# Cached keys stored head channel first by the host: attention and memory keys loaded in place instead of transposed on the tensor engine

## The chip, the cores and the metric

The kernel runs on one core of one Trainium2 chip. The metric is device time in microseconds (us) of one execution; smaller is better. The host may lay out the inputs as it likes before the launch, and that is not timed. Engines are named as in the profile: PE (TensorE, with PEld for its weight loads), DVE (VectorE), ACT (ScalarE), POOL (GpSimd) and SP (SyncE), whose queue issues most DMAs.

## The reference, cut to what matters

One layer of a streaming encoder on two groups of tokens: a prompt of 2048 frames (16 tiles of 128 rows), and 8 short streams ("samples") of 16 new frames each, together one more tile of 128 rows. Only the samples have caches, and their keys are what the change is about.

```python
# mixer attention of a sample: 256 cached frames + 16 new ones, 8 heads x 64
k_ext = concat([past_k, k]);  v_ext = concat([past_v, v])
s = einsum("bqhd,bkhd->bhqk", q, k_ext) * 64**-0.5 + bias
p = softmax(s);  att = einsum("bhqk,bkhd->bqhd", p, v_ext)

# cross-attention of a sample into its 256 cached memory tokens, 4 heads x 256
s = einsum("bthd,bmhd->bhtm", h @ w_mq, cache_mem_k) * 256**-0.5
o = einsum("bhtm,bmhd->bthd", softmax(s), cache_mem_v)
```

Both scores contract over the head channel d. A PE matmul contracts over the 128 partitions, so the keys have to lie with d on the partitions and the cached frames along the row. The caches come with frames first: cache_att_k is 8 x 256 frames x 512 channels, cache_mem_k is 8 x 256 tokens x 1024 channels.

## The kernel before, in words

The phases follow each other: memory keys and values of the prompt, projections with the convolution (`phase_proj`), prompt attention (`attention`), output projection (`mixout`), cross-attention (`phase_cross`), and the feed-forward layers. The whole program passes through a scheduler that plans with costs of its own and sets the order on each engine, so the order on an engine isn't that of the code; each engine then runs its row of instructions strictly in that order, and SP's DMA issues are such a row too.

SBUF is cut by hand into regions. A `Region` gives a tag its places, and `t(...)` walks round them. Two regions matter here. `att_pools` lays the samples' tiles from 34.5 KB of the arena `sbF`: `kc` (2 x 4 KB, raw keys), `kt` (1 x 4.25 KB, transposed keys with 16 new columns), `pp`, `vn` (1 x 2 KB). In the same arena the projection phase keeps the convolution's inputs `ut` (six slots of 3.125 KB from 26 KB; the last group's four channel blocks j = 0 to 3 take the slots at 32.25, 35.375, 38.5 and 41.625 KB) and `us`, the samples' conv input (44.75 to 50.5 KB, a quarter for each j). So the first loads of the attention phase wait for the last taps of the convolution, on DVE (`conv_vector`, L523) for `ut`, on ACT (L532) for `us`.

`attention` runs 8 heads x 16 tiles ("units"). A unit has score matmuls (L861), a fused bias-and-maximum on DVE (L793), the exponential on ACT (L795), transposes of the probabilities on PE (L878) with eviction and split on ACT and DVE (L879, L880), and after each four units the value matmuls (L891). Beside head h runs `sample(h)` as filler, one step at every second unit: load keys, values and new values (L800, L802, L804); eight PE transposes of 128x128 in two steps (L812), each four evicted by an ACT copy (L813); the new frames' keys by POOL (L815); score matmuls (L826); softmax; transposes of the probabilities (L835); value matmuls with 32 columns (L844, L845).

`mixout` multiplies 17 tiles by w_out as products of split fp32 (high and low part, three matmuls each, helper `mm3h`, L291). Beside it `cross_sample` runs as filler: query projection; then 16 jobs of keys (8 samples x 2 halves of the heads), then 16 jobs of values, then the output projection. `Ahead` makes each job two ahead of its use. A key job before: the first half's job loads both 128-token blocks of the sample (two tiles `wf`, 512 KB each, L1091); per block four transposes (L1170) into PSUM, a high part by an ACT cast from PSUM (L1172), a low part by a DVE subtraction of it from PSUM (L1173); then eight score matmuls (L1189). A value job needs no transpose: `split(load(...))` loads 512 KB into `wf`, casts it on ACT (L1085) and subtracts on DVE (L1086), both from SBUF.

Of the kernel before, what the change touches and what calls it, by code (L numbers as in the profile page):

```python
# [17 lines left out]
P = 128  # L18
D = 1024
# [6 lines left out]
NM = 256  # L26
# [3 lines left out]
DEC_B = 8  # L30
DEC_S = 16
PAST = 256
# [104 lines left out]
class Build:  # L137
# [610 lines left out]

    def att_pools(self):
        sbF, sbR, fa, fb = self.sbF, self.sbR, self.fa, self.fb  # L750
        self.attp = (Region().lay(sbF, 34.5, ("kc", 4, 2), ("kt", 4.25, 1), ("pp", 1.5, 1), ("vn", 2, 1))
                     .at("z", 2.5, (fa, [24]), (fb, [0, 2.5, 5]), (fa, [9, 11.5, 14, 16.5]))
                     .lay(fb, 7.5, ("vc", 4, 2), ("nmx", 0.03125, 12), ("sm", 0.03125, 2))
                     .lay(fa, 0, ("qbd", 2.5, 2), ("otmp", 2, 1), ("bs", 1.0625, 1)).lay(fa, 19, ("bt", 2.5, 2))
                     .lay(sbR, 0, ("q20", 8, 1), ("k20", 8, 1), ("kl0", 8, 1), ("q21", 8, 1), ("k21", 8, 1), ("kl1", 8, 1),
                          ("v20", 8, 1), ("ph1", 10, 1), ("pl1", 10, 1), ("v21", 8, 1))
                     .lay(sbR, 88, ("ph0", 10, 1), ("pl0", 10, 1)))
# [25 lines left out]
    def attention(self):  # L783
        nc, A = self.nc, self.A
# [11 lines left out]
            return z  # L796

        def sample(s):
            kc = self.t(pool, [P, 2, 512], F32, "kc", 2)
            nc.sync.dma_start(kc[:, :, :], A["cache_att_k"][s].rearrange("(b p) d -> p b d", p=P))  # L800
            vc = self.t(pool, [P, 2, 512], F32, "vc", 2)
            nc.sync.dma_start(vc[:, :, :], A["cache_att_v"][s].rearrange("(b p) d -> p b d", p=P))  # L802
            vn = self.t(pool, [DEC_S, 512], F32, "vn", 2)
            nc.sync.dma_start(vn[:, :], self.vsamp[s * DEC_S:(s + 1) * DEC_S, :])  # L804
            yield
            kt = self.t(pool, [P, 4, PAST + DEC_S], F32, "kt", 1)
            for c2 in range(0, 4, 2):
                pt = self.t(ps_t, [P, 2, 2, P], F32, "t")
                for c in range(2):
                    for b in range(2):  # L810
                        cc = slice((c2 + c) * P, (c2 + c + 1) * P)
                        nc.tensor.transpose(pt[:, c, b, :], kc[:, b, cc], self.ident[:, :])  # L812
                nc.scalar.copy(kt[:, c2:c2 + 2, :PAST].rearrange("p c (b k) -> p c b k", k=P), pt[:, :, :, :])  # L813
                yield
            nc.gpsimd.tensor_copy(kt[:, :, PAST:], self.ksamp[:, :, s * DEC_S:(s + 1) * DEC_S])  # L815
            yield
            qb = qbds[s % 2]
            for o in range(2):
                rr = slice(o * DH, (o + 1) * DH)
                nc.vector.tensor_copy(qb[rr, :, o * DEC_S:(o + 1) * DEC_S],  # L820
                                      self.qsamp[rr, :, s * DEC_S:(s + 1) * DEC_S])
            qb = qb[:, :, :].rearrange("p c x -> p (c x)")
            n = PAST + DEC_S
            ps = self.t(ps_s, [P, 2, 512], F32, "s")[:, 0, :n]
            for c in range(4):
                nc.tensor.matmul(ps, qb[:, c * P:(c + 1) * P], kt[:, c, :], start=c == 0, stop=c == 3)  # L826
            sm = self.t(pool, [P, 1], F32, "sm", 2)
            z = softmax_band(ps, n, bs[:, :], sm[:, :])
            nc.vector.reciprocal(sm[:, :], sm[:, :])
            nc.gpsimd.tensor_scalar(z[:, :n], z[:, :n], sm[:, :], None, ALU.mult)  # L830
            yield
            pt = self.t(ps_t, [P, 3, P], F32, "t")
            for b in range(3):
                w = P if b < 2 else DEC_S
                nc.tensor.transpose(pt[:w, b, :], z[:, b * P:b * P + w], self.ident[:, :])  # L835
            pp = self.t(pool, [P, 3, P], F32, "pp", 1)
            nc.scalar.copy(pp[:, :2, :], pt[:, :2, :])
            nc.scalar.copy(pp[:DEC_S, 2, :], pt[:DEC_S, 2, :])
# [230 lines left out]
    def cross_sample(self, pool, ps_so, ps_p):  # L1069
# [19 lines left out]
        def load(src):  # L1089
            wf = self.t(pool, [P, D], F32, "wf")  # L1090
            nc.sync.dma_start(wf[:, :], src)  # L1091
            return wf
# [63 lines left out]

        z = self.t(pool, [P, MH, NM], F32, "sh", 1)
        jobs = [(s, b) for s in range(DEC_B) for b in range(2)]
        kcs = {}

        def keys(s, half):
            if half == 0:
                kcs[s] = [load(A["cache_mem_k"][s, b * P:(b + 1) * P, :]) for b in range(2)]
            kh = self.t(pool, [P, 4, NM], F32R, "kvh")
            kl = self.t(pool, [P, 4, NM], F32R, "kvl")
            for b in range(2):
                bs = slice(b * P, (b + 1) * P)
                pt = self.t(ps_p, [P, 4, P], F32, "p")
                for k in range(4):
                    nc.tensor.transpose(pt[:, k, :], kcs[s][b][:, (4 * half + k) * P:(4 * half + k + 1) * P],  # L1170
                                        self.ident[:, :])
                nc.scalar.copy(kh[:, :, bs], pt[:, :, :])  # L1172
                nc.vector.tensor_tensor(kl[:, :, bs], pt[:, :, :], kh[:, :, bs].bitcast(F32), ALU.subtract)  # L1173
            return kh, kl

        ahead = Ahead([lambda j=j: keys(*j) for j in jobs])
        pd = pad(0, qT)
# [1 line left out]
        for x, (s, half) in enumerate(jobs):  # L1179
            kh, kl = next(ahead)  # L1180
            cur = pd
# [4 lines left out]
            for k in range(4):  # L1186
                kk = 4 * half + k
                for y, r in enumerate((kh, kl)):
                    nc.tensor.matmul(sc[:, kk // 2, :], cur[:, kk, :], r[:, k, :],  # L1189
                                     start=s % 4 == 0 and kk % 4 == 0 and y == 0,  # L1190
                                     stop=s % 4 == 3 and kk % 4 == 3 and y == 1, skip_group_check=True)
            if half == 1 and s % 4 == 3:
# [454 lines left out]
def layout(inputs):  # L1647
# [8 lines left out]
    o["cache_att_k"] = i["cache_att_k"].reshape(DEC_B, PAST, 512)  # L1656
    o["cache_att_v"] = i["cache_att_v"].reshape(DEC_B, PAST, 512)
    o["cache_conv"] = i["cache_conv"].reshape(DEC_B * HALO, 512)
    o["cache_mem_k"] = i["cache_mem_k"].reshape(DEC_B, NM, D)
    o["cache_mem_v"] = i["cache_mem_v"].reshape(DEC_B, NM, D)  # L1660

    def colblocks(w):
# [39 lines left out]
```

## Time and profile before

| | |
|---|---|
| median of three runs | 3033.25 us (3031.68 to 3037.04) |
| profiled execution | 3033.59 us, its span 3031.8 us |
| PE busy | 2949.8 us (97%), PEld 2715.4 us (90%) |
| DVE, ACT, POOL busy | 2138.1 (71%), 1357.7 (45%), 1397.0 us (46%) |
| mean granted PE clock | 0.987 of full speed |
| DMA | 500.08 MB, 165 GB/s over the span |

In windows of the profile a row gives, for a stretch of time, each engine's busy us with its instruction count, then the granted clock, the busy share of the 16 DMA engines, and GB/s. In groups and lines of instructions a row gives line, engine, operation, output<-input, count, busy time and mean ns of one, and what ended the idle time before it. A matmul record's length has a pipeline tail in it, so the busy time of a group of back-to-back matmuls divided by their count gives their pace, and the mean of one doesn't.

### The profile page before, as it was taken

The numbers are of one execution on the slowest core, as the hardware profiler recorded it, in microseconds if no ns is written. First come the engines' busy times: TensorE is split into PE (matmuls) and PEld (weight loads), VectorE is DVE, ScalarE is ACT, GpSimd is POOL, SyncE is SP. The second block draws the span as 40 slices with busy tenths as digits, with TensorE's granted clock in tenths as the row PEclk, the third lists the DMA queues.
The fourth block names the chain that finished last, engine by engine and source line by source line (L and its number), as shares of the span: only waits on it lengthen the run. The fifth ranks groups of instructions, "written<-read, shape, count | busy, mean of one in ns | idle before, by whom it ended". The sixth has DMA issues, their size and how long they took to land.

```text
span 3031.8 us, 45992 instructions
## 1 busy us (share of the span) xinstructions
PE 2949.8 (97%) x16924; PEld 2715.4 (90%) x16924; DVE 2138.1 (71%) x3077; ACT 1357.7 (45%) x2718; POOL 1397.0 (46%) x1304
## 2 busy tenths in 40 slices
PE   8999999979999999999999999999999999999998
PEld 8999999969997888787888999999999999888786
DVE  6696895957775466535357887888788998656655
ACT  4545454757784345323234333433334444433433
POOL 0267495710012234325356655555555776424413
PEclk9999999989999999999999999999999999999999
DMA  8635255557753556324246433544334446756654
GB/s 300 245 110 188 87 161 163 169 142 182 170 145 134 176 183 227 125 66 144 78 167 216 138 133 119 180 161 160 139 130 153 145 139 208 255 172 208 222 196 163
DMA packets 196429, 500.08 MB, mean 165 GB/s; under 512 B 18981, under 2 KB 82989, under 8 KB 187875
## 3 DMA queue, kind: packets, MB, share of 16 engines
q1 hardware_dynamic: 185883, 461.09, 47.3%
q0 software_dynamic: 10320, 36.05, 3.1%
q8 instruction: 133, 2.18, 0.3%
q14 instruction: 93, 0.76, 0.1%
HBM read 365.97 MB, written 141.81 MB: 167 GB/s over the span
## 4 chain that ended last, share of the span: by engine, by line
PE 40%; DMA 3%; DVE 3%; POOL 2%; issue 1%; ACT 1%; SPq 0%; DVEq 0%; POOLq 0%; ACTq 0%
PE psb L285 13%; PE psb L284 13%; PE psb L283 13%; DMA sbf<-in_w_down_dram 1%; PE psb L291 1%; DMA sbf<-x 1%; POOL sbf L1553 1%; DVE sbr L1614 1%; PE psb L1408 1%; DMA sbf<-hn 0%; DVE sbr L1431 0%; POOL sbf L340 0%; DMA hn<-sbf 0%; DVE flexb L1493 0%; DMA sbf<-in_w_gate_dram 0%
## 5 line engine op out<-in xcount | busy, mean ns | idle before, releaser
L283 PE MATMUL psb<-sbr 128*128 128x384 f32 (+3 forms) x2808 | 943.3, 337 | 4.4 <-ACT sbr L1613 1.4
L284 PE MATMUL psb<-sbr 128*128 128x384 f32 (+3 forms) x2356 | 806.8, 343 | 2.7 <-DVE sbr L320 2.4
L285 PE MATMUL psb<-sbr 128*128 128x512 f32 (+3 forms) x1848 | 633.2, 344 | 3.5 <-DVE sbr L1614 3.4
L283 PEld LDWEIGHTS psb<-sbr 128*128 128x128 f32 x2808 | 531.2, 189 | 34.4 <-ACT sbr L1613 2.8
L285 PE MATMUL psb<-sbr,sbx 128*128 128x384 f32 (+2 forms) x1484 | 477.8, 323 | 0.0
L284 PEld LDWEIGHTS psb<-sbr 128*128 128x128 f32 x2356 | 445.8, 189 | 29.8 <-DVE sbr L320 2.7
L285 PEld LDWEIGHTS psb<-sbr 128*128 128x128 f32 x1848 | 348.1, 189 | 33.3 <-DVE sbr L1614 6.6
L291 PE MATMUL psb<-sbr 128*128 128x512 f32 x1200 | 296.1, 395 | 6.4 <-DVE sbr L1019 1.7
L1431 DVE TENSOR_TENSOR sbr<-sbf,sbr 128x512 fp32r<-128x512 f32 x258 | 263.1, 1023 | 39.7 <-ACT sbr L1430 38.8
L1430 ACT CAST sbr<-sbf 128x512 fp32r<-128x512 f32 x258 | 159.3, 620 | 276.9 <-PE psb L284 231.0
L285 PEld LDWEIGHTS psb<-sbr,sbx 128*128 128x128 f32 x1484 | 281.5, 190 | 0.2
L291 PEld LDWEIGHTS psb<-sbr 128*128 128x128 f32 x1200 | 222.8, 189 | 52.9 <-DVE sbr L1019 1.9
L523 DVE SCALAR_TENSOR_TENSOR psb<-sbf,psb 128x768 f32<-128x768 f32 (+1 forms) x290 | 264.3, 911 | 6.2
L1614 DVE TENSOR_TENSOR sbr<-sbf,sbr 128x384 fp32r<-128x384 f32 (+1 forms) x231 | 170.8, 762 | 94.0 <-ACT sbr L1613 92.1
L278 POOL TENSOR_TENSOR sbx<-sbf,sbr 128x1024 fp32r<-128x1024 f32 x60 | 151.6, 2529 | 80.7 <-ACT sbr L277 77.2
L1613 ACT CAST sbr<-sbf 128x384 fp32r<-128x384 f32 (+1 forms) x231 | 111.0, 497 | 168.3 <-PE psb L284 153.7
L1553 POOL TENSOR_TENSOR sbf<-sbf 128x512 f32<-128x512 f32 x77 | 108.0, 1407 | 167.9 <-DMA sbf<-in_w_down_dram 166.1
L533 POOL TENSOR_TENSOR flexb<-flexb,flexb 128x128 f32<-128x128 f32 (+1 forms) x180 | 169.4, 941 | 22.3 <-ACT flexb L532 12.8
L283 PE MATMUL psb<-sbr,sbx 128*128 128x384 f32 (+1 forms) x524 | 170.6, 327 | 1.6 <-ACT sbx L1430 0.9
L1430 ACT CAST sbx<-sbf 128x512 fp32r<-128x512 f32 x153 | 94.7, 621 | 162.4 <-PE psb L284 150.6
L1431 DVE TENSOR_TENSOR sbx<-sbf,sbx 128x512 fp32r<-128x512 f32 x153 | 152.3, 997 | 15.9 <-ACT sbx L1430 15.5
L277 ACT CAST sbr<-sbf 128x1024 fp32r<-128x1024 f32 x98 | 102.7, 1051 | 107.2 <-PE psb L284 57.6
(336 smaller groups left out, 6246.9 us busy)
## 6 DMA issues: line engine op xcount, KB each, us to landing
af<-flexb SPq DMA_DIRECT2D x33, 1344.0 KB, 6.0
sbf<-in_w_down_dram SPq DMA_DIRECT2D x154, 256.0 KB, 3.8
sbf<-af SPq DMA_DIRECT2D x90, 384.0 KB, 3.9
sbf<-in_w_gate_dram SPq DMA_DIRECT2D x66, 512.0 KB, 3.4
sbf<-in_w_up_dram SPq DMA_DIRECT2D x66, 512.0 KB, 3.4
sbf<-x SPq DMA_DIRECT2D x49, 512.0 KB, 3.9
sbf<-in_w_in_dram SPq DMA_DIRECT2D x48, 512.0 KB, 4.1
sbr<-ks SPq DMA_DIRECT2D x28, 512.0 KB, 10.2
```

What stands on the lines that cost most here:

```text
L278: self.lo_engine.tensor_tensor(lo[:, :], wf[:, :], hi[:, :].bitcast(F32), ALU.subtract)
L283: nc.tensor.matmul(ps, lh, rh, start=start, stop=False, **kw)
L284: nc.tensor.matmul(ps, lh, rl, start=False, stop=False, **kw)
L285: nc.tensor.matmul(ps, ll, rh, start=False, stop=stop, **kw)
L291: nc.tensor.matmul(y[o], l, r[:, o * 512:(o + 1) * 512], start=start and x == 0, stop=stop and x == 2)
L523: nc.vector.scalar_tensor_tensor(acc if w < CW - 1 else o, src(w), cwt[:, j, w:w + 1], acc, ALU.mult, ALU.add)
L533: nc.gpsimd.tensor_tensor(o, o, v, ALU.add)
L1430: nc.scalar.copy(hs[j][:, :], src[j])
L1431: nc.vector.tensor_tensor(ls[j][:, :], src[j], hs[j][:, :].bitcast(F32), ALU.subtract)
L1553: nc.gpsimd.tensor_tensor(acc[:, :], acc[:, :], q[:, :], ALU.add if s > 0 else ALU.subtract)
L1613: nc.scalar.copy(ch[:, m], a[:, x, m])
L1614: nc.vector.tensor_tensor(cl[:, m], a[:, x, m], ch[:, m].bitcast(F32), ALU.subtract)
```

## The change: what it does

The host writes the cached keys with the channels first. cache_att_kt[s] is 128 channels x (4 channel blocks x 256 frames); cache_mem_kt[s, half] is 128 channels x (4 channel blocks x 256 tokens). The kernel loads them straight into the place where the transposes used to put them.

```diff
-        self.attp = (Region().lay(sbF, 34.5, ("kc", 4, 2), ("kt", 4.25, 1), ("pp", 1.5, 1), ("vn", 2, 1))
+        self.attp = (Region().lay(sbF, 34.5, ("kt", 4.25, 2), ("pp", 1.5, 1), ("vn", 2, 2))
...
         def sample(s):
-            kc = self.t(pool, [P, 2, 512], F32, "kc", 2)
-            nc.sync.dma_start(kc[:, :, :], A["cache_att_k"][s].rearrange("(b p) d -> p b d", p=P))
+            kt = self.t(pool, [P, 4, PAST + DEC_S], F32, "kt", 2)
+            nc.sync.dma_start(kt[:, :, :PAST], A["cache_att_kt"][s].rearrange("p (c k) -> p c k", k=PAST))
...
             yield
-            kt = self.t(pool, [P, 4, PAST + DEC_S], F32, "kt", 1)
-            for c2 in range(0, 4, 2):
-                pt = self.t(ps_t, [P, 2, 2, P], F32, "t")
-                for c in range(2):
-                    for b in range(2):
-                        cc = slice((c2 + c) * P, (c2 + c + 1) * P)
-                        nc.tensor.transpose(pt[:, c, b, :], kc[:, b, cc], self.ident[:, :])
-                nc.scalar.copy(kt[:, c2:c2 + 2, :PAST].rearrange("p c (b k) -> p c b k", k=P), pt[:, :, :, :])
-                yield
             nc.gpsimd.tensor_copy(kt[:, :, PAST:], self.ksamp[:, :, s * DEC_S:(s + 1) * DEC_S])
...
         def keys(s, half):
-            if half == 0:
-                kcs[s] = [load(A["cache_mem_k"][s, b * P:(b + 1) * P, :]) for b in range(2)]
-            kh = self.t(pool, [P, 4, NM], F32R, "kvh")
-            kl = self.t(pool, [P, 4, NM], F32R, "kvl")
-            for b in range(2):
-                bs = slice(b * P, (b + 1) * P)
-                pt = self.t(ps_p, [P, 4, P], F32, "p")
-                for k in range(4):
-                    nc.tensor.transpose(pt[:, k, :], kcs[s][b][:, (4 * half + k) * P:(4 * half + k + 1) * P],
-                                        self.ident[:, :])
-                nc.scalar.copy(kh[:, :, bs], pt[:, :, :])
-                nc.vector.tensor_tensor(kl[:, :, bs], pt[:, :, :], kh[:, :, bs].bitcast(F32), ALU.subtract)
-            return kh, kl
+            return split(load(A["cache_mem_kt"][s, half])[:, :])
...
-                    nc.tensor.matmul(sc[:, kk // 2, :], cur[:, kk, :], r[:, k, :],
+                    nc.tensor.matmul(sc[:, kk // 2, :], cur[:, kk, :], r[:, k * NM:(k + 1) * NM],
```

The `kt` tile now has two places and receives the DMA itself, in 1 KB pieces (a row of 256 frames; the tile's rows are 272 long), where `kc` came in 2 KB pieces. `vn` has two places too. `sample` has two filler steps fewer. The lines behind the cut move up: L826 is L817 in the new kernel, L861 L852, L878 L869, L891 L882, L1085 and L1086 are L1076 and L1077, L1189 is L1167.

The scheduler plans anew from the cut on. First place: PE in the key jobs beside `mixout` (L291 is w_out, L1170 the transposes, L1189 the scores). Before:

```order
L1170 MATMUL psb<-ident_73,sbf 128x128 x4
L1189 MATMUL psb<-flexb_8732 128x256 x7
L1189 MATMUL psb<-sbr,flexb_8732 128x256
L291 MATMUL psb<-sbr 128x512
L965 MATMUL psb<-ident_73,sbr 16x128
L1189 MATMUL psb<-sbr,flexb_8732 128x256 x7
L291 MATMUL psb<-sbr 128x512 x3
L1170 MATMUL psb<-ident_73,sbf 128x128 x4
L291 MATMUL psb<-sbr 128x512
L291 MATMUL psb<-sbr,sbx 128x512 x7
```

And now (L1167 is L1189 of before, L956 is L965):

```order
L956 MATMUL psb<-ident_73,sbr 16x128
L291 MATMUL psb<-sbr 128x512 x12
L1167 MATMUL psb<-flexb_8652 128x256 x8
L291 MATMUL psb<-sbr 128x512 x6
L1167 MATMUL psb<-sbr,flexb_8652 128x256 x8
L291 MATMUL psb<-sbr 128x512 x6
```

The transposes between the blocks of w_out are gone, and a job's eight score matmuls stand in one piece between them.

Second place: PE in a later head of `attention`, around the transposes of sample 2's keys before, and its scores now.

```order
L878 MATMUL psb<-ident_73,flexb_157 128x128
L861 MATMUL psb<-sbr 128x384 x2
L812 MATMUL psb<-ident_73,sbf 128x128 x4
L861 MATMUL psb<-sbr 128x384 x2
L861 MATMUL psb<-sbr 128x256 x2
L878 MATMUL psb<-ident_73,flexb_157 128x128 x4
```

And now:

```order
L882 MATMUL psb<-sbr 128x384 x2
L817 MATMUL psb<-sbf,flexb_153 128x272 x4
L852 MATMUL psb<-sbr 128x256 x2
L869 MATMUL psb<-ident_73,flexb_153 128x128 x3
L882 MATMUL psb<-sbr 128x512
```

The sample's scores (L817) take the place in the head where the transposes stood, and the units around them are shuffled.

Third place: SP's queue at the end of `phase_proj`, where the first sample's loads stand among the stores of q and k (L717) that free the projection's output tiles. Before:

```order
L717 DMA ks_15_87<-sbf 128x2x384
L717 DMA ks_15_87<-sbf 128x2x128
L717 DMA qs_11_83<-sbf 128x2x384
L717 DMA qs_11_83<-sbf 128x2x128
L717 DMA ks_16_88<-sbf 128x2x384
L717 DMA ks_16_88<-sbf 128x2x128
L717 DMA qs_12_84<-sbf 128x2x384
L804 DMA sbf<-vsampd_149 16x512
L717 DMA qs_12_84<-sbf 128x2x128
L800 DMA sbf<-in_cache_att_k_dram 128x2x512
```

And now:

```order
L717 DMA ks_15_87<-sbf 128x2x384
L804 DMA sbf<-vsampd_149 16x512
L800 DMA sbf<-in_cache_att_kt_dram 128x4x256
L717 DMA ks_15_87<-sbf 128x2x128
L717 DMA qs_11_83<-sbf 128x2x384
L717 DMA qs_11_83<-sbf 128x2x128
L717 DMA ks_16_88<-sbf 128x2x384
L717 DMA ks_16_88<-sbf 128x2x128
L717 DMA qs_12_84<-sbf 128x2x384
L717 DMA qs_12_84<-sbf 128x2x128
L800 DMA sbf<-in_cache_att_kt_dram 128x4x256
```

The first key load stood 18 rows above this piece before, behind the stores of v; now it stands with a load of `vn` ahead of seven stores. The second key load keeps its place behind them.

More of the change, by code (lines that the diff above doesn't have):

```diff
@@ L1158, in cross_sample @@
         jobs = [(s, b) for s in range(DEC_B) for b in range(2)]
-        kcs = {}
         def keys(s, half):
-            if half == 0:
-                kcs[s] = [load(A["cache_mem_k"][s, b * P:(b + 1) * P, :]) for b in range(2)]
-            kh = self.t(pool, [P, 4, NM], F32R, "kvh")
-            kl = self.t(pool, [P, 4, NM], F32R, "kvl")
-            for b in range(2):
-                bs = slice(b * P, (b + 1) * P)
-                pt = self.t(ps_p, [P, 4, P], F32, "p")
-                for k in range(4):
-                    nc.tensor.transpose(pt[:, k, :], kcs[s][b][:, (4 * half + k) * P:(4 * half + k + 1) * P],
-                                        self.ident[:, :])
-                nc.scalar.copy(kh[:, :, bs], pt[:, :, :])
-                nc.vector.tensor_tensor(kl[:, :, bs], pt[:, :, :], kh[:, :, bs].bitcast(F32), ALU.subtract)
-            return kh, kl
+            return split(load(A["cache_mem_kt"][s, half])[:, :])
         ahead = Ahead([lambda j=j: keys(*j) for j in jobs])
@@ L1658, in layout @@
     o["cache_conv"] = i["cache_conv"].reshape(DEC_B * HALO, 512)
-    o["cache_mem_k"] = i["cache_mem_k"].reshape(DEC_B, NM, D)
+    o["cache_att_kt"] = i["cache_att_k"].reshape(DEC_B, PAST, 4, P).transpose(0, 3, 2, 1).reshape(DEC_B, P, D)
+    o["cache_mem_kt"] = i["cache_mem_k"].reshape(DEC_B, NM, 2, 4, P).transpose(0, 2, 4, 3, 1).reshape(DEC_B, 2, P, D)
     o["cache_mem_v"] = i["cache_mem_v"].reshape(DEC_B, NM, D)
```

## The prediction

> **What bounds the kernel now.** I read the page's first two parts, then windows of the two stages that the change touches, then the rows of what it removes.
>
> ```profile
> PE 2949.8 (97%) x16924; PEld 2715.4 (90%) x16924; DVE 2138.1 (71%) x3077; ACT 1357.7 (45%) x2718; POOL 1397.0 (46%) x1304
> ```
>
> PE is busy nearly all the time, but that is a mean. By stage (attention runs from about 645 to 930 us, the samples' memory keys from 1027 to 1104 us):
>
> ```profile
> 650.00:700.00 50.00, 40.35 (x246) 36.57 (x245) 29.86 (x75) 31.31 (x78) 2.81 (x6) 0.86 0.69 175
> 700.00:750.00 50.00, 50.00 (x344) 46.99 (x344) 41.22 (x99) 41.66 (x98) 2.71 (x6) 0.97 0.70 179
> 750.00:800.00 50.00, 50.00 (x333) 47.14 (x332) 37.10 (x90) 37.49 (x89) 1.79 (x6) 0.93 0.76 177
> 800.00:850.00 50.00, 50.00 (x338) 47.14 (x336) 38.66 (x92) 39.49 (x92) 2.70 (x6) 0.93 0.59 152
> ...
> 1020.00:1060.00 40.00, 40.00 (x231) 33.72 (x230) 19.70 (x30) 14.58 (x31) 10.97 (x22) 1.00 0.51 175
> 1060.00:1110.00 50.00, 50.00 (x301) 42.84 (x300) 29.18 (x48) 20.92 (x44) 16.50 (x33) 1.00 0.56 185
> ```
>
> In the key jobs PE has no gap, DVE works half of the time (19.7 of 40 and 29.2 of 50 us) and the clock is full: PE alone sets the pace. In attention after 700 us PE has no gap either, but DVE and ACT are at 75 to 83%, so I looked whom they wait for (690 to 870 us; total, times, longest):
>
> ```profile
> DVE flexb L793 <- PE psb L861: 15.7, 18, 2.2
> ...
> ACT sbr L879 <- PE psb L878: 17.7, 17, 4.1
> ```
>
> They wait for PE. Only at the start of attention (650 to 700 us, PE 40.35 of 50) does something else decide.
>
> **The change part by part.** What it removes from PE, with the busy time of each group, which for back-to-back matmuls is what they occupy:
>
> ```profile
> L1170 PE MATMUL psb<-ident,sbf 128*128 128x128 f32 x128 | 18.5, 273 | 0.0
> L812 PE MATMUL psb<-ident,sbf 128*128 128x128 f32 x64 | 10.2, 284 | 5.3 <-ACT sbf L813 5.1 <-ACT flexb L553 0.2
> ```
>
> That is 18.5 / 128 = 0.145 us for one key transpose and 10.2 / 64 = 0.159 us for an attention one, 28.7 us in all. No cheaper matmul takes their place: scores and shapes stay.
>
> Memory keys. All 128 stand in the gap-free stage, so I count 18.5 us. Around them ACT and DVE change:
>
> ```profile
> L1172 ACT CAST sbr<-psb x20: 578/587/593, 1034.1 to 1097.4; 128x512 fp32r<-128x512 f32 x20
> ...
> L1085 ACT CAST sbr<-sbf x22: 1036/1050/1057, 948.3 to 1207.4; 128x1024 fp32r<-128x1024 f32 x22
> ...
> L1173 DVE TENSOR_TENSOR flexb<-psb,flexb x12: 678/691/692, 1029.0 to 1104.6; 128x512 fp32r<-128x512 f32 x12
> ...
> L1086 DVE TENSOR_TENSOR flexb<-sbf,flexb x10: 1212/1226/3422, 955.9 to 1211.1; 128x1024 fp32r<-128x1024 f32 x10
> ```
>
> A job's two casts of 587 ns become one of 1050, its two subtractions of 691 ns one of 1226: ACT gains 16 x 0.12 = 2 us and DVE 16 x 0.16 = 2.5 us, off the path, so nothing. But the new subtraction has a bad case. The PSUM form never took more than 693 ns, the SBUF form up to 3422. One instance in this stage shows why:
>
> ```profile
> 1024.81 0.69 DVE L1019 TENSOR_TENSOR sbx<-flexb,sbx 128x512 fp32r<-128x512 f32 x1 [1.42 <-ACT sbx L1018]
> ...
> 1029.15 2.39 POOL L1062 TENSOR_TENSOR flexb<-flexb 128x1024 f32<-128x1024 f32 x1 [1.05 <-DVE flexb L1061]
> 1029.58 2.51 DVE L1019 TENSOR_TENSOR sbx<-flexb,sbx 128x512 fp32r<-128x512 f32 x1
> ```
>
> The same DVE instruction takes 0.69 us alone and 2.51 beside a POOL operation of 2.39 us. The Trainium skill, page "SBUF — State Buffer" (its rule on the shared port pair), says it outright: a tensor_tensor with two SBUF inputs contends with GpSimd's reads, and the later one is blocked for the whole instruction; the trace agrees (2.51 against 0.69 us). So the change moves 16 subtractions from a form that this cannot hit to one that it can. The job is made two ahead of its use, and DVE has half its time free, which covers it. What leaks through is bounded from the 32 existing SBUF splits of this phase; PE's waits for them between 940 and 1320 us are
>
> ```profile
> PE psb L291 <- DVE flexb L1086: 0.8, 1, 0.8
> PE psb L291 <- DVE sbx L1086: 0.4, 1, 0.4
> ```
>
> 1.2 us for 32, so 0.6 us for 16: a cost of 0.6, with 0 as the lower end; the upper end is a rival below.
>
> The loads of memory keys stay 512 KB each in rows of 4 KB. The value jobs already load in just the new manner, and land in 4.0 us, so I cost them at nothing:
>
> ```profile
> sbf<-in_cache_mem_v_dram SPq DMA_DIRECT2D x16, 512.0 KB, 4.0
> ...
> sbf<-in_cache_att_k_dram SPq DMA_DIRECT2D x8, 512.0 KB, 5.6
> flexb<-in_cache_att_v_dram SPq DMA_DIRECT2D x8, 512.0 KB, 12.1
> ```
>
> The attention keys come in 1 KB pieces now. No row shows that price; between 5.6 us (the 2 KB keys) and 12.1 us (the slowest cache load here) any landing is hidden, since a key load is issued long ahead: the first at 567.1, the last at 836.8 us, while the transposes that use them run at 652.4 and 904.3:
>
> ```profile
> L800 SPq DMA_DIRECT2D sbf<-in_cache_att_k_dram x8: 373/386/578, 567.1 to 836.8; - x8
> ...
> L812 PE MATMUL psb<-ident,sbf x64: 270/273/477, 652.4 to 904.3; 128*128 128x128 f32 x64
> ```
>
> The leads are 85 and 67 us. The new wait: the load for sample s+2 needs the scores of sample s (L826), where it needed the transposes of s. SP did wait for those:
>
> ```profile
> SPq L800 <- PE psb L812: 10.1, 4, 7.5
> ```
> ```profile
> 662.23 2.05 PE L826 MATMUL psb<-sbf,flexb 128*128 128x272 f32 x8
> ```
>
> Behind that load stand the next head's q, k and v on SP, and PE waits for them at the head's turn. The new order puts the scores in the head where the transposes stood, so the wait stays as it is, 10.1 us in four; were it to grow by the few us between the two (662.2 us against 652.4, the start of the first transposes, for the first sample), the next head's loads would still have most of a head of some 35 us (645 to 930 over eight). I cost it at nothing.
>
> Attention. The 16 ACT copies of 586 ns go too (9.4 us), off the path while PE leads. Of the 64 transposes, 56 lie in the PE-bound heads; the first sample's eight stand where PE waits:
>
> ```profile
> 652.39 0.66 PE L812 MATMUL psb<-ident,sbf 128*128 128x128 f32 x4 [0.23 <-ACT flexb L553]
> ...
> 656.66 0.28 ACT L691 ACTIVATE sbf<-psb 128x128 fp32r<-128x128 f32 x1 [3.34 <-DMA qs<-sbf]
> ...
> 658.16 0.57 ACT L813 COPY sbf<-psb 128x512 f32<-128x512 f32 x1
> ...
> 658.79 1.12 PE L812 MATMUL psb<-ident,sbf 128*128 128x128 f32 x4 [5.09 <-ACT sbf L813]
> ```
>
> PE's wait of 5.09 us is put down to the copy L813, but ACT itself stood until 656.66, in L691, for the store of q. L691 is still there, and evictions (L879) that PE needs are ordered behind it. So the wait changes its name: I count 0, with 5.1 as the other end, and leave out these eight (0.66 + 1.12 = 1.8 us): 10.2 - 1.8 = 8.4. Another wait of PE on L813 (0.6 us, by scores L826) goes for good.
>
> SP's queue. `vn` and the first key load now stand ahead of seven stores that go out from 590.9 us. The new `kt` place (34.5 to 38.75 KB) overlaps the conv inputs of j = 0, 1 and the edge of 2; the second `vn` place (46.5 to 48.5 KB) the quarters j = 1 and 2 of `us`. The last taps of j = 2 (on ACT counted back 30 from the last, the taps of j = 3):
>
> ```profile
> 588.37 0.74 DVE L523 SCALAR_TENSOR_TENSOR flexb<-sbf,psb 128x512 f32<-128x512 f32 x1
> 588.80 0.40 ACT L532 ACTIVATE flexb<-sbf 128x128 f32<-128x128 f32 x1 [0.34 <-POOL flexb L533]
> ...
> 590.89 1.05 SPq L717 DMA_DIRECT2D ks<-sbf  x2
> ...
> 616.56 0.37 SPq L800 DMA_DIRECT2D sbf<-in_cache_att_k_dram  x1
> ```
>
> Both are over by 589.2, before SP gets there, so the queue isn't held: 0.
>
> Sum: 18.5 + 8.4 + 0.6 - 0.6 = 26.9 us. The profiled execution took 3033.6 us, 0.3 above the median: 3033.6 - 26.9 = 3006.7, and by the median 3006.3. I say 3006.
>
> **Rivals.**
>
> More than the sum. If the 5.1 us wait goes with its eight transposes (1.8), the sum is 33.8 us and the time 2999.5. The clock could add to it. In the rows above it is 0.86, 0.97, 0.93 and 0.93 in attention; the lost time from 650 to 850 us is 50 x (0.14 + 0.03 + 0.07 + 0.07) = 15.5 us. Were half of that tied to what the samples put between the units, up to 8 us more would come back: 2991.5. Against it: in the key jobs, with twice as many transposes in less time, the clock is 1.00. The Trainium skill, "TensorE: Matmul & The Clock Gate", Part 4, has a transpose not count as busy for the gate, which speaks for this rival; the 1.00 beside 128 transposes doesn't bear it out here.
>
> Less: DVE takes over in the key jobs. DVE had 48.9 us of work in 1020 to 1110. Without the 32 PSUM subtractions (22.1) and with 16 at the worst 3.42 (54.7), it has 81.5 us, in a stage that PE alone would finish in 90 - 18.5 = 71.5. Ten of the 18.5 us would go: 3016. It needs a POOL operation beside each split, while POOL is busy 27.5 of 90 us. The same figure results if attention gives nothing, DVE and ACT being close behind: 3033.3 - 18.5 = 3014.8.
>
> No change, within 0.2% (6 us, what a measurement of this kernel can tell): both losses and a worse order at the start of attention together, 3027 to 3039.
>
> Slower: SP is held after all, at the load of `kt` ahead of the seven stores, until the conv's last tap, as the second key load was: from 590.9 to 616.6, 25.7 us. The projection's outputs have two tiles, so ACT and then PE would stand for it, and the clock fall as at 650 us. With a few us of that, the 26.9 gain is gone: 3034 and more. It decides only if the wait is for j = 3, past 615 us; the places say j = 2.
>
> **How the numbers follow.** The sum holds with 0.60 (3000 to 3012 as its own range: the two ends of the 5.1 us wait, and some us of reshuffled order); more than that 0.16; less, 0.16, at 3012 to 3024; same 0.04; slower 0.04. Leaving out a tenth at either end gives 2994 to 3019. Faster by over 0.2% are the first three: 0.92.
>
> **What would show it.** Right: no transposes with `sbf` as input at 1027 to 1104 us, PE gap-free there, and the 16 jobs some 18 us shorter; heads after the first about 1.2 us shorter each. Wrong, by step: PE waits on L1077 (the new number of L1086) in the key jobs, with splits of 2 us and more; PE gaps in the heads with DVE or ACT named; a pause of SP before the L717 stores at 591 us; a wait for `in_cache_att_kt`. The prediction fails most easily by the order: the whole program from 640 us on is planned anew, and the start of attention has some 10 us of PE waits in it that can move either way.

## The result, and the profile after

| kernel | median, us (runs) | kernel before beside it | ratio, 95% interval |
|---|---|---|---|
| changed | 3015.83 (5: 3012.05 to 3021.98) | 3031.68 | 0.9949, 0.9932 to 0.9966 |
| changed, on another chip | 3013.44 (5: 3009.40 to 3021.62) | 3033.53 | 0.9937, 0.9924 to 0.9949 |

The change makes the kernel faster by 15.9 us, and by 20.1 in the second comparison (differences of medians). The forecast was 3006, a gain of 27; about two thirds of it came. By the profiled executions the gain is 3031.8 - 3014.0 = 17.8 us of span. The page's first part:

```profile
PE 2927.9 (97%) x16732; PEld 2695.0 (89%) x16732; DVE 2133.1 (71%) x3061; ACT 1348.7 (45%) x2686; POOL 1394.9 (46%) x1304
```

PE has 192 matmuls fewer, as it should. The windows that answer to those of before:

```profile
650.00:700.00 50.00, 37.41 (x204) 33.00 (x203) 26.47 (x66) 26.31 (x65) 2.51 (x4) 0.80 0.64 159
700.00:750.00 50.00, 49.99 (x330) 47.25 (x327) 40.54 (x97) 39.27 (x94) 2.99 (x8) 0.93 0.72 180
750.00:800.00 50.00, 49.88 (x348) 46.89 (x348) 41.26 (x102) 39.88 (x94) 2.02 (x7) 1.00 0.78 185
800.00:850.00 50.00, 49.84 (x345) 47.20 (x344) 41.24 (x97) 40.70 (x94) 2.46 (x5) 0.97 0.71 183
850.00:900.00 50.00, 46.88 (x307) 42.68 (x306) 37.98 (x91) 38.79 (x87) 8.41 (x6) 0.97 0.55 144
...
1020.00:1060.00 40.00, 40.00 (x212) 33.35 (x211) 27.17 (x32) 17.94 (x33) 16.68 (x35) 1.00 0.60 201
1060.00:1110.00 50.00, 50.00 (x267) 42.05 (x266) 30.04 (x44) 22.09 (x45) 20.89 (x34) 1.00 0.60 198
```

The key jobs look as forecast: PE without a gap, full clock, DVE at 60 to 68%. Attention doesn't: from 650 to 700 us PE works 37.4 us where it worked 40.35, and from 850 to 900 it is idle for 3.1 us, where before it was for 0.7:

```profile
850.00:900.00 50.00, 49.28 (x324) 45.98 (x324) 39.34 (x97) 39.80 (x89) 8.62 (x7) 0.93 0.56 151
```

To say where the time went, I cut the program at events: "attention" from 28 us after the last convolution tap (L523) to the last value product (L891, now L882), "mixout" from there to the last store of x1. One row for each, before:

```profile
643.70:945.90 302.20, 287.82 (x1869) 264.92 (x1868) 220.75 (x522) 221.69 (x514) 27.19 (x39) 0.94 0.62 160
945.90:1220.00 274.10, 264.64 (x1368) 219.50 (x1367) 160.25 (x202) 114.97 (x215) 106.67 (x155) 0.98 0.57 187
```

and after:

```profile
644.50:943.20 298.70, 280.60 (x1801) 257.25 (x1801) 220.05 (x520) 215.05 (x495) 27.17 (x39) 0.94 0.63 161
943.20:1201.20 258.00, 249.45 (x1242) 205.86 (x1242) 160.64 (x187) 112.57 (x198) 107.23 (x155) 0.99 0.60 199
```

Mixout got 16.1 us shorter, attention 3.5. What comes before (+0.8 us at the last tap) and behind (1811.8 and 1812.8 us to the end of the span) is the same within 1 us. In attention PE's busy time fell by 7.2 us, and its idle time grew from 14.4 to 18.1.

### The profile page after: what moved, and what is told of

The parts are those of the page before. It is cut to its first block, busy times and chain, and to the rows that moved or that the text cites. A ratio compares the mean times of both kernels' runs of the same rounds, so it can differ in the third digit from the quotient of the medians.

```text
span 3014.0 us, 45557 instructions
## 1 busy us (share of the span) xinstructions
PE 2927.9 (97%) x16732; PEld 2695.0 (89%) x16732; DVE 2133.1 (71%) x3061; ACT 1348.7 (45%) x2686; POOL 1394.9 (46%) x1304
## 4 chain that ended last, share of the span: by engine, by line
PE 38%; DMA 4%; POOL 3%; issue 3%; DVE 2%; ACT 1%; SPq 0%; DVEq 0%; POOLq 0%; ACTq 0%
PE psb L285 12%; PE psb L284 12%; PE psb L283 12%; DMA sbf<-in_w_down_dram 2%; POOL sbf L1531 1%; PE psb L291 1%; DMA sbf<-x 1%; DMA sbf<-hn 1%; PE psb L1386 1%; DVE sbr L1592 0%; POOL sbf L340 0%; DVE sbr L1535 0%; DVE sbr L1409 0%; DMA sbf<-in_w_gate_dram 0%; DMA hn<-sbf 0%
## 5 line engine op out<-in xcount | busy, mean ns | idle before, releaser
L291 PE MATMUL psb<-sbr 128*128 128x512 f32 x1200 | 293.6, 394 | 3.1 <-DVE sbr L278 1.1
L523 DVE SCALAR_TENSOR_TENSOR psb<-sbf,psb 128x768 f32<-128x768 f32 (+1 forms) x290 | 264.4, 912 | 6.2
L291 PEld LDWEIGHTS psb<-sbr 128*128 128x128 f32 x1200 | 222.4, 189 | 49.3 <-DVE sbr L278 1.5
L1592 DVE TENSOR_TENSOR sbr<-sbf,sbr 128x384 fp32r<-128x384 f32 (+1 forms) x231 | 162.8, 727 | 98.8 <-ACT sbr L1591 95.2
L533 POOL TENSOR_TENSOR flexb<-flexb,flexb 128x128 f32<-128x128 f32 (+1 forms) x180 | 167.1, 929 | 21.8 <-ACT flexb L532 12.3
L277 ACT CAST sbr<-sbf 128x1024 fp32r<-128x1024 f32 x98 | 102.5, 1049 | 110.0 <-PE psb L284 56.5
```

Source lines behind the costliest of these rows:

```text
L291: nc.tensor.matmul(y[o], l, r[:, o * 512:(o + 1) * 512], start=start and x == 0, stop=stop and x == 2)
L523: nc.vector.scalar_tensor_tensor(acc if w < CW - 1 else o, src(w), cwt[:, j, w:w + 1], acc, ALU.mult, ALU.add)
L533: nc.gpsimd.tensor_tensor(o, o, v, ALU.add)
L1592: nc.vector.tensor_tensor(cl[:, m], a[:, x, m], ch[:, m].bitcast(F32), ALU.subtract)
```

## The experiments

Each stage is taken apart in the same way for every profiled execution: its length, PE's idle time in it, the time lost to the clock (over pieces of 10 us, length times one minus the granted clock), and the rest, which is PE's work at full clock. "Start" is the idle time in the first 62 us of attention, "end" that after its first 206 us; between them PE is idle 0.0 to 0.3 us in every kernel. Each row is one profiled execution; the times further down are medians over several.

| kernel | attention | idle (start, end) | clock | rest | mixout | idle | clock | rest |
|---|---|---|---|---|---|---|---|---|
| before | 302.2 | 14.4 (11.2, 3.1) | 18.7 | 269.1 | 274.1 | 9.5 | 4.2 | 260.4 |
| mem_only | 298.2 | 12.8 (10.6, 2.2) | 15.3 | 270.1 | 258.4 | 9.4 | 3.4 | 245.6 |
| tr_x3 | 302.9 | 13.7 (12.3, 1.4) | 20.5 | 268.7 | 301.7 | 9.4 | 4.4 | 287.9 |
| before_bias | 292.2 | 9.7 (9.6, 0.1) | 13.6 | 268.9 | 274.2 | 9.4 | 4.2 | 260.6 |
| changed | 298.7 | 18.1 (14.2, 3.6) | 18.7 | 261.9 | 258.0 | 8.5 | 2.0 | 247.5 |
| after_again | 307.9 | 17.9 (13.3, 4.3) | 29.0 | 261.0 | 258.0 | 8.6 | 2.0 | 247.4 |
| att_only | 298.7 | 19.1 (14.3, 4.5) | 18.8 | 260.8 | 272.4 | 8.6 | 2.2 | 261.6 |
| bias_early | 295.6 | 16.0 (10.8, 5.2) | 17.1 | 262.5 | 260.2 | 9.4 | 5.2 | 245.6 |
| two_steps | 300.9 | 13.1 (12.1, 0.9) | 27.2 | 260.6 | 258.1 | 8.2 | 3.2 | 246.7 |
| wout_free | 294.7 | 16.6 (14.0, 2.3) | 17.1 | 261.0 | 257.8 | 8.5 | 2.0 | 247.3 |
| both | 294.6 | 10.9 (7.8, 3.0) | 22.1 | 261.6 | 260.2 | 9.3 | 5.2 | 245.7 |
| both_again | 293.2 | 12.7 (10.0, 2.7) | 18.7 | 261.8 | 260.1 | 9.5 | 6.6 | 244.0 |
| both_steps | 293.5 | 12.4 (10.8, 1.7) | 18.8 | 262.3 | 260.5 | 11.1 | 4.8 | 244.6 |

The first four kernels have the samples' attention as it was, the others the changed one. Inside each kind attention's rest holds within 2 us. Mixout's kinds go by the memory keys: before, before_bias and att_only transpose them, tr_x3 does so three times over, the other nine kernels load them; inside a kind the rest holds within 3.5 us. The clock column goes from 13.6 to 29.0 us in attention. Idle time at a lowered clock stands in both the idle and the clock column, so attention's rest is 1.1 to 2.8 us too small and mixout's by up to 1.7; where it matters, the sum that counts such time once is given too.

**What is a transpose worth?** tr_x3 is the kernel before with

```diff
-                for k in range(4):
+                for k in (0, 1, 2, 3) * 3:
                     nc.tensor.transpose(pt[:, k, :], kcs[s][b][:, (4 * half + k) * P:(4 * half + k + 1) * P],
```

> The kernel before with each of the 128 memory-key transposes issued three times into the same PSUM place, so 256 more in the stage where PE has no gap; nothing else is changed, and the results are the same. Theory 'busy time' (the forecast's): a transpose costs what its group's busy time gives, 18.5 / 128 = 0.145 us, so +37 us, about 3069. Theory 'start to start': of each run of four only the time until the next matmul starts counts (0.36 us where the row says 0.60, since the last record's tail lies under the next matmul), 0.095 us each over 126 of them, so +24 us, about 3057. A result of 3054 to 3061 speaks for the second, 3065 to 3073 for the first. ACT and DVE get no work, so if the time grows by less than 20 us, PE isn't the bound there.

3059.20 us (4 runs) beside 3033.53: ratio 1.0089 (1.0076 to 1.0102), +25.7 us or 0.100 each; the interval is 0.090 to 0.121. Mixout's rest grew by 27.0, 0.105 each. So 0.145 us as the price of one transpose is out, and 3059.20 lies in the range of "start to start". But this run can't tell whether a group is to be priced by its starts or by its busy time: the new transposes stand inside the old runs and make no new run. In the two traces the busy time of the transposes grows from 18.5 to 45.4 us (+26.9), and by starts they grow from 12.0 to 40.1 (+28.2). What the end of a run is worth is seen in the rows of before. PE in the key jobs there (start, busy time):

```profile
1046.25 0.60 PE L1170 MATMUL psb<-ident,sbf 128*128 128x128 f32 x4
1046.61 0.36 PE L1189 MATMUL psb<-sbx,flexb 128*128 128x256 f32 x1
1046.81 0.28 PE L1189 MATMUL psb<-sbr,flexb 128*128 128x256 f32 x1
1046.92 0.28 PE L1189 MATMUL psb<-sbx,flexb 128*128 128x256 f32 x1
```

Four transposes have a busy time of 0.60 us, but the next matmul starts 0.36 us after the first of them. In tr_x3:

```profile
1050.53 1.47 PE L1170 MATMUL psb<-ident,sbf 128*128 128x128 f32 x12
1051.76 0.36 PE L1189 MATMUL psb<-sbr,flexb 128*128 128x256 f32 x1
```

Twelve take 1.23 us start to start, 0.103 each, with the same tail of 0.24 behind them. Over the 128 transposes of before the starts give 12.0 us, 0.093 each (the expectation's 0.095 divides the same sum by 126), and over the 64 in attention 6.6 us, 0.104 each. The busy time of a group has one tail for each run, and a run of four is 40% tail. A run costs something behind it too: the first score matmul after it takes 0.20 us to the next start, where the second takes 0.11.

The Trainium skill has the tail and the pace in "TensorE: Matmul & The Clock Gate", Part 2, "Back-to-back issue gap" and the steps before it: the drain of a matmul lies under the fill of the next, and a sustained stream of matmuls at 128 columns goes at about 81 ns each. The traces, at 0.093 to 0.105 us for these fp32 transposes, are nearer to that than to the 0.145 that I took.

**The two parts alone.** mem_only has the change in the memory keys only (`keys` and the score line), att_only in `sample` and the region only.

> Only the memory keys come channel first; the samples' attention keys are loaded and transposed as before. The forecast's term for this part is 18.5 us of transposes, +0.6 for the DVE splits: 3032 - 17.9 = about 3014. In the whole change the stretch from the first mixout product to the last cross output gained 13 to 16 us by the two traces, so if each part simply adds up, 3015 to 3019. Theory 'start and end of attention' (the attention part gives back what it saves): this kernel is as fast as the whole change, 3014 to 3018, and its attention phase ends where it did before (last value products at 946 us, within 1.5 us). Rival 'the rest is a loose reshuffle': its attention, too, ends some us off from before, since the plan after the cut is made anew in any case.

> Only the attention keys come channel first; memory keys are loaded and transposed as before. Forecast's term: 8.4 us of transposes and 0.6 of a wait, so 3032 - 9 = 3023. Theory 'start and end': the first heads fall back by 7 to 9 us (sample 0 reaches its scores two steps early, DVE stands for the bias table until about 671 us), the middle heads win 12 to 13 us, the last head and the step to mixout lose 2 to 4: attention ends 1 to 4 us earlier and the time is 3028 to 3031. If instead the attention part by itself gives its full 9 us, the loss in the whole change comes from both parts together.

mem_only took 3014.42 us (6 runs) beside 3032.89: 0.9943 (0.9925 to 0.9961), -18.5. att_only took 3027.83 (12 runs): 0.9987 (0.9974 to 1.0000), -5.1. The memory keys alone are as fast as the whole change; the attention part adds little that a median can show. That mem_only came out at the 3014 that the forecast's 18.5 us give is partly chance: in its profile mixout got 15.7 us shorter, and attention, in which nothing was removed, 4.0, with 3.4 less lost to the clock, 1.6 less idle and 1.0 more rest. Its attention ended 4.5 us earlier than before, where the theory had it within 1.5, so its rival was right that an end time alone proves nothing. In att_only the idle time is that of the whole change, 19.1 us against 18.1 and 17.9: it comes with the attention part. And its rest is 8.3 us under that of before (7.2 with idle time at a low clock counted once). So the attention part does save 7 to 8 us of work and gives 5 back.

**Where PE stands at the start.** PE's waits from 640 to 712 us, before:

```profile
PE psb L861 <- DVE flexb L793: 5.2, 4, 3.4
PE psb L812 <- ACT sbf L813: 5.1, 1, 5.1
```

and after:

```profile
PE psb L852 <- DVE flexb L793: 7.7, 5, 3.6
PE psb L852 <- ACT flexb L695: 4.5, 1, 4.5
PE psb L869 <- ACT flexb L553: 1.5, 1, 1.5
```

The wait of 5.1 us changed its name, as forecast. The waits on DVE's maximum (L793) grew by 2.5 us, and that on L553, 0.2 us before, by 1.3. On DVE stands (start, length, idle before it):

```profile
667.95 1.28 DVE L871 TENSOR_TENSOR sbr<-psb,sbr 128x512 fp32r<-128x512 f32 x2
673.07 0.44 DVE L793 CUSTOM_DVE_ANT_0 flexb<-psb,flexb 128x272 f32<-128x272 f32 x1 [3.84 <-DMA flexb<-toep]
```

This is the pass over sample 0's scores, 272 wide, waiting for its bias table `bs`, which eight DMAs bring (L904 before, L895 now). Before it stood as well, in the same place:

```profile
671.53 0.44 DVE L793 CUSTOM_DVE_ANT_0 flexb<-psb,flexb 128x272 f32<-128x272 f32 x1 [4.28 <-DMA flexb<-toep]
```

The table lies at 7 KB of the arena `fa`, where the projection keeps tiles of its normalization. DVE's last instruction on these, L557, ends at 658.2 us before and 658.3 after, and only then do the eight loads go out:

```profile
658.37 13.06 SPq L895 DMA_DIRECT2D flexb<-toep  x8
```

They take until 671 us, because SP waits ahead of five of them for other loads to land, 10.2 us in all. Three kernels test the place: bias_early (the changed kernel, the table behind `vn` in sbF), two_steps (the changed kernel, with two empty `yield` where the transpose steps were), and before_bias (the kernel before, `vn` and the table from `pp`'s place on and `pp` in fa, so three tiles move). The core of the first:

```diff
-                     .lay(fa, 0, ("qbd", 2.5, 2), ("otmp", 2, 1), ("bs", 1.0625, 1)).lay(fa, 19, ("bt", 2.5, 2))
+                     .lay(fa, 0, ("qbd", 2.5, 2), ("otmp", 2, 1)).lay(fa, 19, ("bt", 2.5, 2))
-        self.attp = (Region().lay(sbF, 34.5, ("kt", 4.25, 2), ("pp", 1.5, 1), ("vn", 2, 2))
+        self.attp = (Region().lay(sbF, 34.5, ("kt", 4.25, 2), ("pp", 1.5, 1), ("vn", 2, 2), ("bs", 1.0625, 1))
```

> The whole change, and the samples' bias tile lies in the samples' own region of sbF, behind the vn tiles, instead of in fa where tiles of the projection's normalization lie; its eight loads no longer need those tiles to be free. Theory 'start': DVE's pass over sample 0's scores (L793, 272 wide) no longer stands for the table until 671 us, the lag of about 9 us at the fourth group of values is gone or is at most half, and the time is 4 to 9 us under the change's: 3007 to 3012. Rival 'later regained': the lag goes but the middle heads then win less, since they were held by other engines; time within 3 us of the change's, 3013 to 3018. Rival 'clock and PE wait there for k and q (the reloads from DRAM)': the lag stays at 6 us or more.

> The changed kernel with two empty steps in each sample's filler, where the two transpose steps were, so that each sample's scores come at the same unit as before. Theory 'two steps early': sample 0's scores no longer stand ahead of the units at the bias table, PE's idle time in the stretch from 28 to 90 us after the last conv tap falls from 14.2 to about 11, and the time is 2 to 5 us under the change's. Theory 'the place of the bias table alone': DVE stands for the table as long as before the steps (until 671 us), but with other work ahead of it; idle 12 to 14 us, time within 3 us. Rival: later scores hold the key load of sample s+2 longer, SP's queue stands, and the time rises by 2 us or more.

> The kernel before, transposes and all, with the bias tile in sbF and pp in fa: does the place of the bias table cost the kernel before anything? Theory 'the change uncovers it': before, PE's 5 us stand for L813 and the eight transposes lie across the same time, so moving the tile gives at most 2 us; PE idle in the stretch from 28 to 90 us after the last conv tap stays at 10 to 11 (10.6 to 12.3 in three executions), time 3030 to 3033. Rival 'it was there all along': idle there falls by 3 us or more, as it did with the change (14.2 to 10.8), and the time by 3 to 6 us, so moving the tile is an edit of its own that owes nothing to the change.

In bias_early the loads of the table go out from 610 us instead of 658, and DVE's stand for it is gone:

```profile
610.44 0.79 SPq L895 DMA_DIRECT2D sbf<-toep  x2
...
662.92 0.44 DVE L793 CUSTOM_DVE_ANT_0 flexb<-psb,sbf 128x272 f32<-128x272 f32 x1 [2.50 <-PE psb L817]
```

Idle at the start falls from 14.2 to 10.8 us; PE's waits on L793 fall from 7.7 to 1.6, and a wait of 2.4 on ACT comes in their place. The time is 3011.45 (5 runs; 0.9929, 0.9915 to 0.9943), 4.4 under the changed kernel's by medians of two comparisons, within the 4 to 9 of the theory, but the intervals don't separate them. The end stretch took 1.6 of the 3.4 us back.

two_steps: idle at the start 12.1, at the end 0.9, in all 13.1; 3011.48 (0.9929, 0.9916 to 0.9942) beside 3013.44 of the changed kernel on the same chip. One of its five executions took 8674.62 us; nothing explains it, and the ratio leaves it out. DVE stood for the table as before, 3.57 us until 670.71. The 2.0 us under the changed kernel are not told apart by the intervals, and with 12.1 us at the start both theories on record stay open. The idle time as a whole, 13.1 us, is in the range of the three executions with the old attention and the old places (12.8 to 14.4), so two steps of filler that do nothing bring back most of the idle time that the shorter `sample` had added, the larger part of it at the end.

before_bias fell to 3023.46 (12 runs) beside 3033.87: 0.9972 (0.9960 to 0.9984), -10.4, more than either theory had. The places cost the kernel before as well, and moving them is an edit of its own; so far the rival was right. Its sign was not there: idle at the start fell from 11.2 to 9.6 us, not by 3 or more, though DVE no longer stands for the table; a wait of 2.4 on DVE's L897 came instead. The other 3.0 us of idle went at the end (3.1 to 0.1), and which of the three moved tiles did that isn't shown. Of its shorter attention (10.0 us) 4.7 are idle and 5.1 clock, so I count 5 as shown.

**Where PE stands at the end.** From 850 to 900 us ACT waits for the first block of w_out (L277 casts it for `mixout`), before and after:

```profile
875.03 1.05 ACT L277 CAST sbr<-sbf 128x1024 fp32r<-128x1024 f32 x1 [0.41 <-DMA sbf<-in_w_out_dram]
```
```profile
867.47 1.05 ACT L277 CAST sbr<-sbf 128x1024 fp32r<-128x1024 f32 x1 [2.98 <-DMA sbf<-in_w_out_dram]
```

The block's staging place (34.5 to 38.5 KB) lies under the first `kt` place, which sample 6's scores now release; the load went out at 862.01 and 870.27 before, so both it and the cast came some 8 us earlier, and the cast waited 2.6 us longer for its data. wout_free moves the samples' tiles up:

```diff
-        self.attp = (Region().lay(sbF, 34.5, ("kt", 4.25, 2), ("pp", 1.5, 1), ("vn", 2, 2))
+        self.attp = (Region().lay(sbF, 38.5, ("kt", 4.25, 2), ("pp", 1.5, 1), ("vn", 2, 1))
```

> The whole change, with the samples' region moved up by 4 KB (kt, pp and one vn place from 38.5 KB), so that the first staging place of w_out (34.5 to 38.5 KB) isn't under a key tile and its load needs no scores of sample 6. Theory 'end': ACT's stand of 3.0 us for w_out at 867 us goes, PE's busy share in 850 to 900 us rises from 46.9 to 48 to 49.5 of 50, and the time is 2 to 4 us under the change's: 3012 to 3014. Rival 'reshuffle': the stand goes, PE has its gaps elsewhere, the time is within 2 us of the change's (3014 to 3018).

ACT's stand is gone (the cast runs at 857.63 with no idle time ahead), and the end's idle time is 2.3 us against 3.6, 4.3 and 4.5 in the three executions with the changed attention and no repair. PE was busy 47.8 of 50 us from 850 to 900, under the 48 that the theory asked for. The time is 3008.19 (6 runs: 3004.36 to 3023.24; 0.9927, 0.9906 to 0.9949), under the theory's 3012 to 3014, which 1 to 2 us of idle time don't explain; the intervals don't part it from the changed kernel. A part of the end's idle time hangs on this wait, 1.3 to 2.2 us; PE's wait of 1.3 us on L871 stayed. two_steps gets 0.9 with the staging place left as it is: there the cast comes 68.5 us before attention ends, against 75.7 in the changed kernel and 70.9 before, and ACT stands for it for 1.09 us. So when the cast comes in ACT's order seems to matter as much as the place; no run changes that order alone.

**The repairs together.** both moves the table and frees the staging place (`kt`, `vn` and `bs` from 38.5 KB, `pp` in fa), both_steps adds the two empty steps, and after_again is the changed kernel.

> The changed kernel once more, on the chip of the other three, to stand beside them: 3013 to 3018 by all theories. If the lag at the start of attention (PE idle 14.2 us in the stretch from 28 to 90 us after the last conv tap, 11.2 before) and ACT's stand of 3.0 us for w_out at 867 us come from the order and the places, they are there again within 1 us; if they were chance of one execution, they are not.

> The changed kernel with both places moved: the samples' keys from 38.5 KB (w_out's first staging place free), one vn place, the bias tile in sbF and pp in fa. From the two single runs (PE idle in the start stretch 14.2 to 10.8 us with the bias tile moved, in the end stretch 3.6 to 2.3 us with w_out's place free): about 5 us less idle than the change, 3009 to 3012. If the places only shift the waits (with the bias tile moved the end stretch went from 3.6 to 5.2), no better than the better of the two: 3008 to 3014.

> Both places moved and the two empty steps. If the three repairs add up: the start stretch at 7.8 us of idle or less, the end stretch at 0.9 instead of 3.0, so 2 us under the version with both places, 3002 to 3005. If the steps and the bias tile repair the same wait: within 2 us of it, 3004 to 3007, idle in attention 11 to 13 us.

> The version with both places moved, once more beside the other two: 3002 to 3008, ratio 0.990 to 0.993 to the kernel before; PE idle in attention 11 to 12 us (10.9 in its first profile, 18 in three of the changed attention without repairs).

after_again: idle 17.9 in attention, ACT's stand for w_out 3.53 us, so both are there again and not chance of one execution. both: 3005.22 (6 runs; 0.9914, 0.9901 to 0.9927) beside 3013.44, 8.2 us faster by medians and under both ranges on record, though the intervals just touch (0.9924 to 0.9949). both_again: 3006.99 (5 runs; 0.9911, 0.9893 to 0.9928). both_steps: 3009.29 (0.9910, 0.9892 to 0.9928), above both ranges on record but the same as both_again within what can be told. Its idle time in attention, 12.4 us, is that of both and both_again (10.9 and 12.7), so the repairs don't add up. They don't repair the same waits, though: PE's 1.5 us for L553 stand in both_again and are gone with the steps, and other waits take their place. The version with both places is the best that was found: 27 to 28 us under the kernel before by medians. before_bias, a like edit of the kernel before, gave 10.4 by itself (5 to 12 by its interval).

## Why the prediction was right, and where it was not

The change did what the prediction said, by the mechanism that it named: transposes left a stage that PE alone paces. But the result, 3015.83 and 3013.44, isn't in the sum's own range of 3000 to 3012; it lies in that of "less", 3012 to 3024, to which the prediction gave 0.16. Two errors of one sign made 27 out of 16 to 20.

**The 18.5 us of the memory keys: mis-sized.** The step "for back-to-back matmuls [the busy time of a group] is what they occupy" failed: the last 0.24 us of each run lie under the next matmul, and in runs of four they are 40%. Measured: mixout's rest falls from 260.9 (mean of before, before_bias, att_only) to 246.0 (mean of the nine with channel-first memory keys), 14.9 us (14.5 with idle time at a low clock counted once). The transposes' starts give 12.0 us of it, and tr_x3's price 0.100 to 0.105 x 128 = 13. Another 0.8 us is in the key scores: start to start the 128 of them take 16.5 us in the three kernels that transpose and 15.7 in mem_only, changed, bias_early and both, where no run of transposes stands ahead of them. What the last 1.7 to 2.1 us are isn't settled.

**The 8.4 us of the attention keys: near in size, but more than half was given back.** All 64 transposes by starts are 6.6 us; attention's rest fell by 7.7 (269.2 to 261.5, means of four and nine kernels), or 7.0 with idle time at a low clock counted once. But idle time rose from 13.6 (mean of before, mem_only, tr_x3) to 18.4 (changed, after_again, att_only): +2.5 us at the start, where sample 0 comes to its scores two steps sooner and the table is no sooner there, and +1.9 at the end. The prediction had the first eight transposes at 0 and the start as the place that could move; it didn't ask what is late next for sample 0 when its transposes go. At the start it was mostly the bias table, in a row of the old trace (4.28 us, above) that I hadn't read: with the table early, start idle is 10.8 us, near the 11.2 of before. The staging place at the end wasn't looked at either.

With the measured sizes: 14.9 + 7.7 - 4.8 = 17.8 us, between the medians' 15.9 and 20.1. That the profiled pair gives 17.8 as well is chance to the tenth: there mixout's rest fell by 12.9, attention's by 7.2, attention's idle grew by 3.7, and mixout lost 3.2 less to idle time and clock, with 1.8 more before and behind.

**The 5.1 us wait counted at 0: right.** It became L852's wait of 4.5 us for L695, which ACT reaches late behind L691.

**DVE's splits, a cost of 0.6: right to within 1 us.** PE's waits for them between 940 and 1320 us, after:

```profile
PE psb L291 <- DVE flexb L1077: 0.7, 1, 0.7
PE psb L291 <- DVE sbx L1077: 0.4, 1, 0.4
```

1.1 us for 48 splits, where 32 had cost 1.2, so nothing was added. Some did take up to 3.43 us, and PE hardly waited for them, as forecast from the two jobs' lead. The rival in which DVE takes over the key jobs is out: PE has no gap there. The rival's other way to its range, "attention gives nothing" (3014.8), lies within 1.4 us of both medians, but its reason, DVE and ACT close behind, is not what was seen: attention gave 7 to 8 us of work and 4.8 of it went into waits at its start and end.

**SP's queue at 0: right in cost, wrong on the wait.** It wasn't to grow from 10.1 us; it did:

```profile
SPq L800 <- PE psb L817: 36.8, 4, 9.7
```

Still, PE was idle for only 0.3 us in the middle of attention, so the key loads and the loads behind them came early enough. SP wasn't held at 591 us (the first key load went out at 592.8), so the slower rival is out too.

**The key loads' landing, hidden: right.**

```profile
sbf<-in_cache_mem_kt_dram SPq DMA_DIRECT2D x16, 512.0 KB, 3.5
...
sbf<-in_cache_att_kt_dram SPq DMA_DIRECT2D x8, 512.0 KB, 8.1
flexb<-in_cache_att_v_dram SPq DMA_DIRECT2D x8, 512.0 KB, 3.7
```

8.1 us for the 1 KB pieces lies between the ends of 5.6 and 12.1, and no engine's wait names this load. Such a figure rests on few loads: the profile has the landing of one of these eight, and the prediction's 5.6 and 12.1 are of two loads each.

**The clock rival: out for the key jobs.** With 384 transposes instead of 128 in tr_x3's key jobs:

```profile
1028.00:1125.00 97.00, 97.00 (x677) 87.71 (x677) 36.86 (x64) 28.05 (x55) 21.56 (x46) 1.00 0.43 141
```

The clock is full. The Trainium skill has a transpose not count as busy for the gate ("TensorE: Matmul & The Clock Gate", Part 4). This stream shows nothing of that, but other matmuls stand between the transposes in it, and no run here has transposes alone. In attention the loss to the clock is 13.6 to 20.5 us with transposes and 17.1 to 29.0 without, so no gain from taking them out shows there.

## What to carry to other kernels

Price a removed matmul by the distance from its start to the next matmul's start, and not by the busy time of its group: short runs carry a tail that lies under the next instruction and doesn't come back. Here the starts (12.0 us, 12.8 with the scores behind) came nearer to the 14.5 to 14.9 measured than the busy time (18.5), but fell short of it. When a step is taken out of a chain that runs beside other work, look for what the next step of that chain waits for, since the chain now gets there sooner; here it was, at the start, a table whose place in memory came free late. And a saving in a stage with two busy helpers is to be read as work and idle time apart, because a single execution's length mixes both with the clock.

## What the runs showed of the hardware that I had not expected

The loss to the clock differs between executions of one and the same kernel, here on two chips: the changed kernel's attention lost 18.7 us in one profile and 29.0 in the other,

```profile
643.10:951.00 307.90, 289.97 (x1805) 266.61 (x1804) 221.23 (x521) 216.17 (x499) 27.20 (x39) 0.91 0.61 157
```

with idle time and work the same to 1 us, and the execution took 3021.62 us where the other took 3015.83. That is as much as most of the effects studied here.

The landing of a 512 KB load can't be read off the size of its pieces here. The attention values come in 2 KB pieces in both kernels, and their known landings went from 11.8 and 12.3 us before to 3.4 to 7.4 (three loads) after. The old keys, in 2 KB pieces too, took 4.1 and 7.1 us, the new ones, in 1 KB pieces, 8.1 (one load). What sets it, the order of the loads or what runs beside them, no run here shows.
